# Pauses, leads and engine changes around the two branches of a hybrid encoder block

## The chip, the cores and the metric

The kernel runs on one core of a Trainium2 chip. A core has a matrix engine (TensorE, PE in the profile), three engines for elementwise work (VectorE or DVE, ScalarE or ACT, GpSimd or POOL), a SyncE (SP) that mostly issues transfers, and DMA engines that move data between memory and the core. Transfers are issued on queues of SP, ACT and POOL. The metric is the device time of one execution in microseconds; lower is better.

## The reference

One layer over a sequence of 2048 rows of width 1024, in fp32:

```python
xn = rmsnorm(x, norm1_g)
z = xn @ w_in                       # 1024 -> 4608 columns
u_pool, zq, zf, zi, zo, zg = split(z)
gates = sigmoid(zg + b_gate).reshape(B, S, 2, D_MODEL)
ya = pool_mixer(u_pool, pool_w, pool_scale) @ w_pa      # 512 -> 1024
yb = hgrn2_mixer(zq, zf, zi, zo, lb, norm_g) @ w_pb     # 512 -> 1024
x = x + (gates[:, :, 0] * ya + gates[:, :, 1] * yb) @ w_o
x = x + conv_glu_ffn(rmsnorm(x, norm2_g), w_up, conv_w, conv_b, w_down)  # 1024 -> 2 x 2816 -> 1024
return rmsnorm(x, final_g)
```

The pool mixer takes trailing means over windows of 2 to 16 rows; the HGRN2 mixer is a gated linear recurrence in chunks of 64 rows; the feed-forward part has a causal convolution of width 3 over the rows and a SiLU gate.

## The kernel before

**Precision.** Each fp32 operand is split in two parts of a shorter type, high and low: a CAST on ACT makes the high part and a subtraction on DVE the low one (L597 and L598 for activations, L205 and L206 for weights). A product is three matmuls: high by high, high by low, low by high. The names end in h and l: `mxs_1h`, `oTs_0l`, `wo_P_0l`, `m_T23h`.

**Products.** Matrix products are done in a Strassen-like form: a 2 x 2 arrangement of parts is combined to seven products P1 to P7 in place of eight. The weights for P4 to P7 are sums of parts of the weight matrix. Some of these sums are built once, in memory: class `Sums` writes, for each group of weight tiles, four matrices s1 to s4 with plain copies (issued by ACT, L278) and accumulating transfers (issued by POOL, L275), each 1 MB or less. The names su0 to su5 belong to the up projection, sd0 to sd2 to the down projection, sw0 to w_o. The generator `prepare` goes through all groups, two at a time, one transfer a step, and is driven by ticks of the matmul stream, one for six matmuls.

**Blocks.** The 2048 rows go through the program as two blocks of 1024 rows, each in two halves of 512 (hf 0 and 1). The second block runs the same code; the sums are built during the first alone. In a block the stages follow each other:

- the input projection (units of `PROJ`, seven products each), with the pooling, the recurrence and the gates beside it;
- branch pa: for each of eight column tiles m, in the order 0, 4, 1, 5, 2, 6, 3, 7, a chain of 12 matmuls for hf 0 and one for hf 1. Its moving operand is the pooled mixture `mx`, stored to memory as `md`, loaded again by SP (L796) and split to `mxs`. DVE multiplies each chain's result by a gate (L1285, L1287) to `ya`;
- branch pb: the same with the output of the recurrence (`od` to `oT` to `oTs`). DVE multiplies by the second gate (`gl`), POOL adds the product to `ya` (L1295) and then, when both halves of a row pair are there, POOL makes the combinations `yf` for P3, P5, P6 and P7 of the next product (L1084, in `add_forms`);
- wo, an object of class `Rows`: seven products of four k-steps. A step needs the split of one tile, `wo_P_k`, and each step multiplies it into four banks of PSUM. DVE adds finished banks to the rows x (L1060);
- up: 22 units of seven products (P1, P2 collect in the bank set X, P6, P7, P4 in Z, P5, P3 in V), with the convolution and the gate after each. `up_order` sets the order: P1 and P2 of two units (called heads), then of the next two, then the other products. The forms of the second half's rows (m_t, m_b, m_T11 and so on) are made by `Task`s meanwhile: transposes on PE (L646), a scaling on ACT, combinations on DVE (L703) and POOL, then splits. They may begin when product number GO_AT of up has been reached;
- down, again `Rows`, eleven k-steps for each product, with tiles reloaded from memory (`g_P`, L796 on POOL's queue), and the final norm.

**Weights.** SP loads them in order (`raw`, eight buffers); ACT and DVE split them into `ops` (six buffers, at most four ahead of use). SP's queue also carries `mx`, `oT`, the gates `gl` and more; it issues in the order of the program.

**Order on an engine.** The code is written in an order, and a scheduler with a timeline model then reorders instructions on each engine by its own estimate of when operands are ready. What each engine executes is therefore read from the printed order.

## Time and profile before

| | us |
|---|---|
| median of three runs | 2626.42 (2625.76 to 2626.61) |
| the profiled execution | 2626.91 |
| its span, first to last instruction | 2625.2 |
| PE busy, 97% of the span | 2537.5 |
| PE idle | 87.7 |
| DVE, ACT, POOL busy | 1977.9, 1170.8, 913.0 |
| mean granted clock of TensorE | 0.987 |

Rows of groups and of the timeline name the line, the engine, the operation, and out<-in by the program's names without buffer numbers. In a timeline row the first number is the start in us, the second the time it lasts, and the bracket at the end is the engine's idle time before it with what released it. ACTq and SPq are the DMA issues of ACT and SP. A matmul of 128 x 512 lasts 0.39 us but the next starts after 0.23, since they are pipelined. In the waits view a row says which engine and tile waited for which other, with total us, times, and the longest.

### The profile page before, as it was taken

What the parts mean: (1) busy time and instruction counts of PE and PEld (TensorE: products, weight loads), DVE (VectorE), ACT (ScalarE), POOL (GpSimd) and SP (SyncE); (2) the same over time, 40 slices, a digit from 0 to 9 for tenths busy, and PEclk for the clock granted to TensorE, in tenths of its full rate; (3) what the DMA queues carried; (4) which work ended last, traced back from release to release, by engine and by line L of the source; (5) the groups of instructions that cost most, each with busy time, mean ns of one, the idle gap of its engine ahead of it and who ended that gap; (6) DMA issues with size and microseconds to landing.
All of it is one profiled execution on the core that took longest, in us unless ns stands there. A gap on an engine that the chain in (4) does not pass through costs nothing. (4 is left out here: it accounts for less than half of the span.)

```text
span 2625.2 us, 35598 instructions
## 1 busy us (share of the span) xinstructions
PE 2537.5 (97%) x11464; PEld 2065.1 (79%) x11464; DVE 1977.9 (75%) x3390; ACT 1170.8 (45%) x2204; POOL 913.0 (35%) x1253
## 2 busy tenths in 40 slices
PE   7899999998999999999999999999999999999998
PEld 6688877777778888878878788888787888887887
DVE  7888779458789877877376787775778887777845
ACT  5334334313655454455364344443345454444633
POOL 6544344042444433353141111210623433335402
PEclk8999999999999999999999999999999999999999
DMA  6787759988768897488364344346452444445942
GB/s 213 271 223 205 204 181 245 267 263 209 217 184 244 239 235 211 148 299 282 98 206 159 97 125 133 109 153 213 149 166 88 151 151 148 141 140 182 378 142 105
DMA packets 254059, 496.90 MB, mean 189 GB/s; under 512 B 26736, under 2 KB 43248, under 8 KB 253552
## 3 DMA queue, kind: packets, MB, share of 16 engines
q1 hardware_dynamic: 187968, 319.89, 38.3%
q0 software_dynamic: 41504, 110.64, 16.5%
q10 hardware_dynamic: 24400, 64.08, 7.0%
q8 instruction: 91, 1.49, 0.2%
q14 instruction: 96, 0.79, 0.1%
HBM read 384.94 MB, written 187.17 MB: 218 GB/s over the span
## 5 line engine op out<-in xcount | busy, mean ns | idle before, releaser
L205 ACT CAST ops<-raw 128x512 fp32r<-128x512 f32 x732 | 451.5, 620 | 819.7 <-PE dn_P L145 140.0
L206 DVE TENSOR_TENSOR ops<-raw,ops 128x512 fp32r<-128x512 f32 x732 | 565.2, 776 | 205.3 <-ACT ops L205 194.3
L1375 DVE SCALAR_TENSOR_TENSOR e<-h,cols,e 128x512 f32<-128x512 f32 x176 | 142.6, 813 | 30.2 <-ACT e L1373 26.1
L1373 ACT ACTIVATE e<-h,cols 128x512 f32<-128x512 f32 x176 | 142.5, 814 | 24.2 <-DVE h L978 16.9
L1378 DVE SCALAR_TENSOR_TENSOR e<-h,cols,e 128x512 f32<-128x512 f32 x176 | 133.9, 769 | 3.0
L796 POOL DMA_DIRECT2D g_P<-dg_P x154 | 83.7, 545 | 107.6 <-PE dn_P L145 69.4
L1084 POOL TENSOR_TENSOR gf_P<-e,e 128x512 f32<-128x512 f32 x44 | 67.9, 1545 | 152.9 <-DVE e L1384 97.5
L1295 POOL TENSOR_TENSOR ya<-ya,gl 128x512 f32<-128x512 f32 x32 | 46.8, 1490 | 107.7 <-DVE gl L1287 107.7
L1084 POOL TENSOR_TENSOR gf_P<-gf_P,e 128x512 f32<-128x512 f32 x44 | 60.2, 1368 | 68.0 <-DVE e L1384 67.5
L1368 POOL COPY h<-h 128x2 f32<-128x2 f32 x88 | 40.7, 481 | 114.3 <-DVE h L976 112.3
L1370 POOL COPY hist<-h 128x2 f32<-128x2 f32 x88 | 35.3, 401 | 125.9 <-DVE h L978 124.2
L1382 ACT ACTIVATE e<-e 128x512 f32<-128x512 f32 x88 | 55.6, 631 | 38.8 <-DVE e L1378 38.4
L1191 POOL TENSOR_TENSOR q<-q,qs 128x512 f32<-128x512 f32 x16 | 21.9, 1366 | 141.6 <-ACT qs L1190 72.9
L978 DVE TENSOR_TENSOR h<-up_u,up_V 128x512 f32<-128x512 f32 x88 | 60.1, 684 | 13.6 <-PE up_V L145 13.1
L1228 ACT ACTIVATE gt<-gt,cols 128x512 f32<-128x512 f32 x48 | 34.8, 725 | 77.4 <-DVE gt L978 63.5
L845 POOL COPY qm<-q 128x64 f32<-128x64 f32 x64 | 24.9, 410 | 117.3 <-DVE q L910 31.2
L1060 DVE TENSOR_TENSOR x<-x,wo_P 128x512 f32<-128x512 f32 x88 | 56.6, 689 | 8.2 <-PE wo_P L145 8.2
L1060 DVE TENSOR_TENSOR ac<-ac,dn_P 128x512 f32<-128x512 f32 x72 | 46.6, 684 | 13.4 <-PE dn_P L145 13.3
L1398 POOL DMA_DIRECT2D dg_P<-gf_P x88 | 52.5, 596 | 10.8 <-POOL gf_P L1084 6.5
L853 PE MATMUL pl<-qm,k 128*128 128x192 f32 x256 | 48.2, 331 | 6.1 <-DVE qm L849 3.8
L1444 POOL TENSOR_TENSOR fss<-fss 128x1 f32<-128x1 f32 x16 | 4.6, 288 | 142.0 <-ACT fj L1433 142.0
L853 PEld LDWEIGHTS pl<-qm,k 128*128 128x128 f32 x256 | 43.3, 191 | 10.4 <-ACT qm L844 3.4
(1265 smaller groups left out, 8283.6 us busy)
## 6 DMA issues: line engine op xcount, KB each, us to landing
g_P<-dg_P POOLq DMA_DIRECT2D x154, 256.0 KB, 6.4
raw<-in_w_up_t SPq DMA_DIRECT2D x132, 256.0 KB, 3.2
raw<-in_w_in_t SPq DMA_DIRECT2D x98, 256.0 KB, 3.2
dg_P<-gf_P POOLq DMA_DIRECT2D x88, 256.0 KB, 3.9
raw<-in_w_io SPq DMA_DIRECT2D x68, 256.0 KB, 5.1
dg_P<-e SPq DMA_DIRECT2D x66, 256.0 KB, 3.3
raw<-in_w_dn SPq DMA_DIRECT2D x66, 256.0 KB, 3.0
x<-in_x SPq DMA_DIRECT2D x64, 256.0 KB, 5.3
```

The costliest lines, as they stand in the source:

```text
L205: self.mark = act.copy(hi, v)
L206: dve.tensor_tensor(lo, v, f32(hi), ALU.subtract)
L796: eng.dma_start(t, d)
L853: pe.matmul(pa_[:, c * 192 : c * 192 + 192], ks[:, (i + c) * P : (i + c + 1) * P], mv[:, c].rearrange("p s x -> p (s x)"), start=True, sto ...
L978: dve.tensor_tensor(dst, t, ps, ALU.add if how == "add" else ALU.subtract)
L1060: dve.tensor_tensor(t, t, ps[j], ALU.add if sg > 0 else ALU.subtract)
L1084: pin(pool.tensor_tensor(t, x0, x1, op))
L1373: in_turn(act.activation(t, h[:, 2:], AF.Identity, bias=col(o_cb + mt), scale=col(o_cw + 4 * MF + mt)))
L1375: in_turn(second(dve.scalar_tensor_tensor(t, h[:, 1 : 1 + TB], col(o_cw + 2 * MF + mt), t, ALU.mult, ALU.add)))
L1378: dve.scalar_tensor_tensor(t, h[:, 0:TB], col(o_cw + mt), t, ALU.mult, ALU.add)
L1382: in_turn(act.activation(g, g, AF.Silu))
L1398: pool.dma_start(d, t)
```

## The change

Six edits.

1. GO_AT is 3 in place of 5: the forms of the second half may begin two products earlier in up.
2. `up_order` leads with P1 of all four heads and then P2 of all four, where P1 and P2 came pair by pair.
3. A flag `quiet` holds `prepare`: while it is set, the generator yields without issuing. It is set when P1 of the last projection unit is through and cleared after branch pb (or when a sum is asked for that isn't done).
4. In `branch`, the first two column tiles run hf 0 of both and then hf 1 of both; the other six are as before.
5. The addition to `ya` and the four combinations `yf` in pb go to DVE; `add_forms` takes the engine as an argument. This is 32 instructions of 128 x 512 a block.
6. The `Rows` object of wo is made before pb, and the splits of P1's first three tiles are made inside pb, at its steps 3, 5 and 7.

```diff
--- before.py
+++ after.py
@@ -60,7 +60,7 @@
 N_SLOTS = 77
 N_RUN = 3
 N_HEADS = 2
-GO_AT = 5
+GO_AT = 3
 LEAD = 5
 X_AT, X_AT2 = 1, 4
 GO_IO = (("P2", 1), ("P2", 0))
@@ -283,6 +283,7 @@
             def src():
                 g, i = self.where[unit]
                 while g not in self.done:
+                    quiet[0] = False
                     prep[0].step()
                 return self.t[g, key][:, i, :]
             return src
@@ -422,7 +423,7 @@
 
     def up_order():
         heads = [(0, 1), (2, 3), (4, 5)][:N_HEADS]
-        res = [(m, p) for ms in heads for p in ("P1", "P2") for m in ms]
+        res = [(m, p) for p in ("P1", "P2") for ms in heads for m in ms]
         res += [(m, p) for ms in heads for p in ("P6", "P5", "P7", "P4", "P3") for m in ms]
 
         rest = [(7 * m + 2 * i, m, p) for m in range(2 * N_HEADS, MF)
@@ -461,7 +462,7 @@
         ms = range(m0, m0 + n + 1)
         return grouped(w_up_t, ms, [MF + m for m in ms], list(range(m0, m0 + n)))
 
-    prep = []
+    prep, quiet = [], [False]
 
     def prepare():
         todo = [sums[name].make(g) for name in ("wo", "up", "dn")
@@ -477,6 +478,8 @@
                 continue
             active.append(g)
             yield lag
+            while quiet[0]:
+                yield 1
 
     def group_rows(src, k0, n):
         v = src[k0 : k0 + n].rearrange("k p c -> p k c")
@@ -1075,13 +1078,14 @@
                         step(j, k, ws[n])
                 stream.used(hold)
 
-    def add_forms(two, forms, k, name, store=lambda p, t: None, sums=True, pin=lambda i: None):
+    def add_forms(two, forms, k, name, store=lambda p, t: None, sums=True, pin=lambda i: None,
+                  eng=pool):
 
         def comb(p, x0, x1, op):
             if (p, k) in forms or x0 is None or x1 is None:
                 return
             t = slot(f"{name}_{p}_{k}")
-            pin(pool.tensor_tensor(t, x0, x1, op))
+            pin(eng.tensor_tensor(t, x0, x1, op))
             forms[p, k] = t
             store(p, t)
 
@@ -1261,22 +1265,36 @@
                 u.multiply(p, forms, late)
                 u.after(p)
                 if n == len(PROJ) - 1 and p == "P1":
+                    quiet[0] = True
                     mtask = Task(pa_task())
 
         def branch(key, s, xs, evac, each):
-            for n, m in enumerate(M_ORDER):
-                each(n)
-                for m2 in M_ORDER[n : n + 3]:
-                    for hf in range(2):
-                        gate(s, m2, hf)
-                w4 = stream.get(key)
+            ws = {}
+
+            def chain(n, hf):
+                m = M_ORDER[n]
+                if n not in ws:
+                    each(n)
+                    for m2 in M_ORDER[n : n + 3]:
+                        for h in range(2):
+                            gate(s, m2, h)
+                    ws[n] = stream.get(key)
+                w4 = ws[n]
+                ps = bank(f"{key}{b0 + hf}_{m}")
+                chain_t(ps, lambda k: (w4[:, 0, k * P : (k + 1) * P],
+                                       w4[:, 1, k * P : (k + 1) * P]),
+                        [xs[hf, k] for k in range(4)])
+                evac(m, hf, gate(s, m, hf), ps)
+                if hf:
+                    stream.used(1)
+
+
+            for hf in range(2):
+                for n in range(2):
+                    chain(n, hf)
+            for n in range(2, len(M_ORDER)):
                 for hf in range(2):
-                    ps = bank(f"{key}{b0 + hf}_{m}")
-                    chain_t(ps, lambda k: (w4[:, 0, k * P : (k + 1) * P],
-                                           w4[:, 1, k * P : (k + 1) * P]),
-                            [xs[hf, k] for k in range(4)])
-                    evac(m, hf, gate(s, m, hf), ps)
-                stream.used(1)
+                    chain(n, hf)
 
         y, yf = {}, {}
 
@@ -1292,11 +1310,11 @@
 
         def evac_b(m, hf, g, ps):
             gated(g, hf, g, ps)
-            pool.tensor_tensor(y[m, hf], y[m, hf], g, ALU.add)
+            dve.tensor_tensor(y[m, hf], y[m, hf], g, ALU.add)
             if m >= KD // 2 and hf:
                 k = m - KD // 2
                 two = {(h, r): y[k + r * (KD // 2), h] for h in range(2) for r in range(2)}
-                add_forms(two, yf, k, f"yf{b0}")
+                add_forms(two, yf, k, f"yf{b0}", eng=dve)
 
         join(mtask)
         otask = []
@@ -1320,7 +1338,15 @@
             for c in range(2):
                 acc[hf, j, c] = xt.pop((("x", b0 + hf), j, c))
 
-        branch("pb", 1, oT, evac_b, load_res)
+        wo = Rows(f"wo{b0}", "wo", OUT, KD // 2, lambda p, k: yf[p, k], acc)
+
+        def each_b(n):
+            load_res(n)
+            if n in (3, 5, 7):
+                wo.make(n // 2)
+
+        branch("pb", 1, oT, evac_b, each_b)
+        quiet[0] = False
 
         def ready_rows(hf):
             def done(j):
@@ -1329,7 +1355,6 @@
                 ready.add((("m", b0 + hf), j))
             return done
 
-        wo = Rows(f"wo{b0}", "wo", OUT, KD // 2, lambda p, k: yf[p, k], acc)
         go_up[0] = False
         for p in ("P1", "P6", "P5"):
             wo.run(p)
```

How the orders move, at three places of block 1. First ACT, at the end of branch pa's start (mxs are the split halves of mx, gt and gd gates, sq the recurrence's norm). Before:

```order
L205 CAST ops_4963<-raw_4650 128x512
L278 DMA su1s_3386<-su1s_3384 16x16384
L791 DMA gd_0_7_4851<-gt_0_7_4849 128x512
L597 CAST mxs_0h<-mx_0_4864 128x512
L205 CAST ops_5017<-raw_4652 128x512
L278 DMA su2s_3514<-su2s_3512 16x16384
L1228 ACTIVATE gt_1_7_4876<-gt_1_7_4876,cols 128x512
L791 DMA gd_1_7_4879<-gt_1_7_4876 128x512
L597 CAST mxs_1h<-mx_1_4892 128x512
```

and now:

```order
L205 CAST ops_4962<-raw_4650 128x512
L794 DMA gd_0_7_4850<-gt_0_7_4848 128x512
L600 CAST mxs_0h<-mx_0_4863 128x512
L205 CAST ops_4986<-raw_4652 128x512
L1232 ACTIVATE gt_1_7_4875<-gt_1_7_4875,cols 128x512
L600 CAST mxs_1h<-mx_1_4891 128x512
L794 DMA gd_1_7_4878<-gt_1_7_4875 128x512
L953 ACTIVATE sq_3_4917,so_3_4918<-po_3_4908 128x128 x4
```

The copies of su1s and su2s are gone from between the casts of the second half's mx tiles; the first of them stands now after the third split of P6 in wo.

Second DVE, from the last chains of branch pb into wo (gl is the gate times the chain's result, ops a weight split, ya and yf as above). Before:

```order
L1287 TENSOR_TENSOR gl_1_7_5586<-gl_1_7_5586,pb_7_5677 128x512
L1285 SCALAR_TENSOR_TENSOR gl_1_7_5588<-gl_1_7_5588,pb_7_5697 128x512
L206 TENSOR_TENSOR ops_5772<-raw_5410,ops_5772 128x512
L598 TENSOR_TENSOR wo_P_0l<-ya_0_5004,wo_P_0h 128x512
L598 TENSOR_TENSOR wo_P_1l<-ya_1_5092,wo_P_1h 128x512
L598 TENSOR_TENSOR wo_P_2l<-ya_2_5195,wo_P_2h 128x512
L598 TENSOR_TENSOR wo_P_3l<-ya_3_5294,wo_P_3h 128x512
L598 TENSOR_TENSOR wo_P_0l<-yf_P_0_5439,wo_P_0h 128x512
```

and now:

```order
L1303 SCALAR_TENSOR_TENSOR gl_1_7_5579<-gl_1_7_5579,pb_7_5691 128x512
L206 TENSOR_TENSOR ops_5754<-raw_5380,ops_5754 128x512
L1313 TENSOR_TENSOR ya_7_5324<-ya_7_5324,gl_1_7_5579 128x512
L1088 TENSOR_TENSOR yf_P_3_5712<-yf_P_3_5710,ya_7_5324 128x512
L601 TENSOR_TENSOR wo_P_3l<-ya_3_5289,wo_P_3h 128x512
L206 TENSOR_TENSOR ops_5775<-raw_5446,ops_5775 128x512
L601 TENSOR_TENSOR wo_P_0l<-yf_P_0_5424,wo_P_0h 128x512
L601 TENSOR_TENSOR wo_P_1l<-yf_P_1_5522,wo_P_1h 128x512
L601 TENSOR_TENSOR wo_P_2l<-yf_P_2_5620,wo_P_2h 128x512
```

Before, all splits of P1 stand after the last chain's result; now `wo_P_3l` alone does, behind one addition and one combination of its own row, and those for the other tiles stand further up.

Third PE, at the start of up (m_t are the transposes of the second half's rows, up_n_X the first products of unit n). Before:

```order
L145 MATMUL up_3_X<-m_f3l,ops_6616 128x512
L145 MATMUL up_3_X<-m_f3h,ops_6616 128x512
L646 MATMUL m_t_6728<-ident,m_xs_0_6459 128x128
L646 MATMUL m_t_6728<-ident,m_xs_0_6509 128x128
L646 MATMUL m_t_6728<-ident,m_xs_0_6542 128x128
L646 MATMUL m_t_6728<-ident,m_xs_0_6581 128x128
L646 MATMUL m_t_6733<-ident,m_xs_1_6460 128x128
L646 MATMUL m_t_6733<-ident,m_xs_1_6510 128x128
L646 MATMUL m_t_6733<-ident,m_xs_1_6543 128x128
L646 MATMUL m_t_6733<-ident,m_xs_1_6582 128x128
L145 MATMUL up_2_X<-m_f4h,ops_6635 128x512
L145 MATMUL up_2_X<-m_f4l,ops_6635 128x512
```

and now:

```order
L145 MATMUL up_3_X<-m_f3l,ops_6565 128x512
L145 MATMUL up_3_X<-m_f3h,ops_6565 128x512
L649 MATMUL m_t_6680<-ident,m_xs_0_6449 128x128
L649 MATMUL m_t_6680<-ident,m_xs_0_6499 128x128
L649 MATMUL m_t_6680<-ident,m_xs_0_6532 128x128
L649 MATMUL m_t_6680<-ident,m_xs_0_6571 128x128
L649 MATMUL m_t_6685<-ident,m_xs_1_6450 128x128
L649 MATMUL m_t_6685<-ident,m_xs_1_6500 128x128
L649 MATMUL m_t_6685<-ident,m_xs_1_6533 128x128
L649 MATMUL m_t_6685<-ident,m_xs_1_6572 128x128
L145 MATMUL up_0_X<-m_f4h,ops_6592 128x512
L145 MATMUL up_0_X<-m_f4l,ops_6592 128x512
```

The same transposes lay behind both halves of units 0 and 1; now the second halves of units 0 to 3 are still to come after them.

## The prediction

> **What bounds the kernel now.** The page first, for the engine that sets the end.
>
> ```profile
> PE 2537.5 (97%) x11464; PEld 2065.1 (79%) x11464; DVE 1977.9 (75%) x3390; ACT 1170.8 (45%) x2204; POOL 913.0 (35%) x1253
> ```
>
> TensorE (PE) is busy 2537.5 of 2625.2 us and the change leaves its 11464 matmuls alone, so all that it can win lies in the 87.7 us in which PE waits, and in matmuls slowed by a lowered clock after a wait. Next the waits of PE, by what it waited for (total, times, longest).
>
> ```profile
> PE wo_P L145 <- DVE wo_P_0l L598: 7.3, 2, 6.7
> PE pa L145 <- ACT mxs_1h L597: 6.3, 1, 6.3
> PE up_Z L145 <- ACT m_T23h L597: 3.7, 2, 1.8
> PE wo_P L145 <- DVE x L1060: 3.0, 2, 1.6
> PE wo_P L145 <- ACT wo_P_0h L597: 2.5, 2, 1.2
> PE pb L145 <- ACT oTs_0h L597: 1.7, 1, 1.7
> PE up_Z L145 <- DVE m_T23l L598: 1.5, 2, 0.8
> PE pb L145 <- ACT oTs_1h L597: 1.0, 1, 1.0
> ```
>
> These eight lie where the change works: branch pa, branch pb, the start of wo, the start of up. Some come once, some twice, and the program runs its two blocks through the same code, so I put the branch stages of block 1 beside those of block 2 (window, length, busy and count of PE, PEld, DVE, ACT, POOL, then granted clock, DMA share, GB/s).
>
> ```profile
> 480.00:540.00 60.00, 53.65 (x231) 42.97 (x230) 23.05 (x42) 16.88 (x40) 4.82 (x6) 0.94 0.88 271
> 540.00:592.00 52.00, 47.88 (x196) 37.33 (x194) 33.15 (x35) 8.37 (x14) 33.48 (x26) 0.97 0.86 275
> 1757.00:1817.00 60.00, 60.00 (x294) 49.80 (x293) 30.48 (x56) 23.13 (x51) 2.41 (x4) 1.00 0.71 230
> 1822.00:1869.00 47.00, 47.00 (x204) 38.05 (x203) 24.43 (x32) 7.16 (x12) 31.47 (x24) 1.00 0.69 230
> ```
>
> In block 2 both branches run without a gap at full clock; in block 1, where alone sum matrices are built, the DMA engines are busier (0.88 and 0.86 against 0.71 and 0.69) and the clock is below 1. 47.00 us for 204 matmuls is 0.230 us a matmul, my unit below; a chain of 12 is 2.8 us.
>
> **Branch pa, block 1.** PE, then the queues that fed it.
>
> ```profile
> 489.62 0.39 PE L145 MATMUL pa<-mxs_0h,ops 128*128 128x512 f32 x1
> 496.35 0.80 PE L145 MATMUL pa<-mxs_1h,ops 128*128 128x512 f32 x1 [6.35 <-ACT mxs_1h L597]
> 500.45 0.63 PE L145 MATMUL pa<-mxs_1h,ops 128*128 128x512 f32 x1
> 501.29 0.39 PE L145 MATMUL pa<-mxs_2l,ops 128*128 128x512 f32 x1
> ```
> ```profile
> 484.78 0.47 ACTq L278 DMA_DIRECT2D su1s<-su1s  x1
> 487.54 0.47 ACTq L278 DMA_DIRECT2D su2s<-su2s  x1
> 495.68 0.62 ACT L597 CAST mxs_1h<-mx 128x512 fp32r<-128x512 f32 x1 [6.90 <-DMA mx<-md]
> 486.57 0.91 SPq L796 DMA_DIRECT2D mx<-md  x1
> ```
>
> The second half's mx tile was issued at 486.57 and cast at 495.68: 9.1 us, in company of two sum copies on ACT's queue. PE idles 6.35 us, then needs 4.94 us (496.35 to 501.29) for ten matmuls and a transpose, about 2.5 in place of 4.94, so 2.5 more: 8.9 in all. The change helps twice: the pause moves both copies behind P1 of wo, and with the first halves of two rows leading PE has one more chain (2.8 us) before it asks for the second half. Without the copies I let the load take half as long, near 4.5 us; with the 2.8 that covers 6.35 with about 1 us over. The third and fourth mx tiles follow close behind, so I leave 0.5: saved 8.4. Bounds: 2.8 if the copies were innocent, 8.9 at best.
>
> **Branch pb, block 1.**
>
> ```profile
> 545.36 0.50 PE L145 MATMUL pb<-oTs_0h,ops 128*128 128x512 f32 x1 [1.73 <-ACT oTs_0h L597]
> 549.71 0.63 PE L145 MATMUL pb<-oTs_0l,ops 128*128 128x512 f32 x1
> ```
>
> The same pattern with oT: with two short DVE waits of 0.2 each, 3.1 us idle, and again slow matmuls (0.63) after it, near 1.4 more: 4.5. Wanted 2.8 us later, two waits of 1.7 and 1.0 vanish whatever the loads do, so I take 4.5; bounds 2.8 and 4.5. The Trainium skill (TensorE: Matmul & The Clock Gate, What's actually happening) has the clock fall only after an idle window of about 3.4 us; the 0.63 rows after waits of 1.7 and 1.0 speak against that, and by it pb would be worth 3.1.
>
> **Start of wo.** Block 1 on PE, then DVE, then POOL; the last three rows are block 2 (DVE, PE, PE).
>
> ```profile
> 592.27 2.09 PE L145 MATMUL wo_P<-ops,wo_P_0h 128*128 128x512 f32 x8 [1.23 <-ACT wo_P_0h L597]
> 601.03 2.07 PE L145 MATMUL wo_P<-ops,wo_P_0l 128*128 128x512 f32 x4 [6.67 <-DVE wo_P_0l L598]
> 607.60 0.63 PE L145 MATMUL wo_P<-ops,wo_P_2h 128*128 128x512 f32 x2
> ```
> ```profile
> 592.52 8.45 DVE L598 TENSOR_TENSOR wo_P_0l<-ya,wo_P_0h 128x512 fp32r<-128x512 f32 x1
> 608.48 0.68 DVE L598 TENSOR_TENSOR wo_P_1l<-yf_P,wo_P_1h 128x512 fp32r<-128x512 f32 x1
> 609.08 0.68 DVE L598 TENSOR_TENSOR wo_P_2l<-yf_P,wo_P_2h 128x512 fp32r<-128x512 f32 x1
> ```
> ```profile
> 592.55 1.80 POOL L1084 TENSOR_TENSOR yf_P<-yf_P,ya 128x512 f32<-128x512 f32 x1
> 600.49 3.30 POOL L1084 TENSOR_TENSOR yf_P<-yf_P,ya 128x512 f32<-128x512 f32 x2
> ```
> ```profile
> 1876.76 1.77 DVE L598 TENSOR_TENSOR wo_P_1l<-ya,wo_P_1h 128x512 fp32r<-128x512 f32 x1
> 1876.89 1.19 PE L145 MATMUL wo_P<-ops,wo_P_0l 128*128 128x512 f32 x4 [0.64 <-DVE wo_P_0l L598]
> 1900.51 0.73 PE L145 MATMUL wo_P<-ops,wo_P_0h 128*128 128x512 f32 x2 [1.62 <-DVE x L1060]
> ```
>
> One split on DVE lasts 8.45 us while POOL adds without a pause; the same split lasts 0.68, one per 0.60 us, once POOL is done. In block 2 it lasts 1.77. So DVE starves beside POOL's adds, and these are what the change takes off POOL. Block 1: 1.23 + 6.67 idle, and 601.03 to 607.60 for 16 matmuls, 6.57 against 3.7: 7.9 + 2.9 = 10.8. Block 2: 1.23 + 0.64 there and 3.0 of waits for x, 4.8.
>
> What DVE takes on: 32 adds a block at 0.60 are 19.2 us. From the first product of pb to P1's last split its order now has 59 instructions, 35.4 us, against 192 matmuls or 44 us of pb, so DVE keeps pace with the chains. Three of P1's four splits stand inside pb; the last is the fifth instruction from the last chain's result, 3.0 us, and PE needs it after three steps of 12 matmuls, 8.3 us. PE's next bank demand is P5's, 22 us into wo; P1's sums end at 11, and their 16 adds with two splits take 10.8 after that where not begun earlier, which they are: about 1.8 us are over. Hidden, then, but thinly. Saved 10.8 + 4.8 = 15.6; bounds 0, if DVE falls behind by as much as it stood still, and 15.6.
>
> **Start of up, each block.** Block 1; block 2 repeats it within 0.01 us.
>
> ```profile
> 713.48 0.49 PE L145 MATMUL up_Z<-m_T23h,ops 128*128 128x512 f32 x1 [1.84 <-ACT m_T23h L597]
> 714.72 0.50 PE L145 MATMUL up_Z<-m_T23l,ops 128*128 128x512 f32 x1 [0.75 <-DVE m_T23l L598]
> 720.70 0.50 PE L145 MATMUL up_V<-m_T12l,ops 128*128 128x512 f32 x1 [0.70 <-DVE m_T12l L598]
> ```
>
> The chain to m_T23 (transposes, m_b, m_t, cast, split) may now start two products earlier, 24 matmuls or 5.5 us, more than 1.84 + 0.75. Four leading heads keep PE on operands that exist meanwhile. T12 stands behind casts and splits of weights that wait for PE's own products, so of its 0.70 I count 0.4, and 0.3 for the slow first matmuls: 3.3 a block, 6.6; bounds 3.7 (m_T23h alone) and 7.6. Later waits of up, for weights and up_u, end with PE's own products and stay.
>
> **What is paid.** The paused copies and adds are all still done. Two kinds now fall elsewhere: su3, su4 into wo and up, and the last sd1, sd2 adds among POOL's loads for down.
>
> ```profile
> g_P<-dg_P POOLq DMA_DIRECT2D x154, 256.0 KB, 6.4
> raw<-in_w_up_t SPq DMA_DIRECT2D x132, 256.0 KB, 3.2
> sd1s<-in_w_dn POOLq DMA_DIRECT2D x4, 1024.0 KB, 11.1
> ```
>
> Weight loads land in 3.2 us with eight raw tiles, eight times 2.8 us, ahead, so in up the transfers are covered by that depth. At the start of down one 11.1 us add goes out just ahead of the first seven g_P loads, on the same queue: between 0 and 11.1 - 6.4 = 4.7 us; I take 1.5, since the loads are issued ahead of need.
>
> **Sum.** 8.4 + 4.5 + 15.6 + 6.6 - 1.5 = 33.6 us. The profiled execution took 2626.91 us (span 2625.2 and 1.7 around it): 2593.3. The median of the runs is 0.5 lower, so I predict 2593. The likeliest case's own range, from part-kept pa and up to a free start of down, is 2588 to 2599.
>
> **Rivals.** (1) The loads stay late: mx's 9.1 us comes from its place on SP's queue, not from the copies. For it: in block 2, without copies, DMA is at 0.71 too. Against: block 2 has no wait. Then pa saves 2.8 and pb 2.8 in place of 12.9: 2600.
>
> (2) DVE is short at its own rate: the 1.8 us of slack in wo go, and each block waits for x at P5 and again at the next banks, 3.0 us as block 2 does now, or twice that: 2593 + 6 to 12, 2599 to 2605. For it: DVE's windows in wo are nearly full already. Against: the 0.60 us spacing.
>
> (3) Down pays: the rings work one queue off in order, so the seven g_P loads wait for the whole add: 4.7 - 1.5 = 3.2 more, twice if the sd2 add catches the next loads: 2596 to 2600. The Trainium skill (DMA: Bandwidth & Descriptors, Queues, rings and completion order) says that of one ring, while different queues share an engine packet by packet; no row of before shows an add ahead of these loads.
>
> (4) Slower: DVE stays as slow with its own adds as beside POOL's. If the 32 adds of pb cost 1.77 each, pb and P1 ask of DVE 35.4 + 32 x 1.17 = 72.8 us against 44 + 5.3 of slack: 23.5 us late a block, 47 in all, with the 15.6 of wo not won: 2593 + 15.6 + 47 = 2656. It turns slower than before once an add costs some 1.3 us. For it: two SBUF inputs as in the starved splits. Against: nothing is left on POOL in pb to starve them but DMA issues.
>
> (5) The pause is void because the sums are forced or forgotten, or the orders come out as before; then near 2625. The printed orders speak against it. A sum group late for its weights would stall SP's queue for tens of us, but the closest group stands some 19 products, 53 us, ahead of its use.
>
> **Chances.** Likeliest 0.62, (1) 0.11, (2) 0.11, (3) 0.08, (4) 0.05, (5) 0.03. What this measurement can tell from no change is 0.2%, 5.3 us. Faster: 0.62 + 0.11 + 0.11 + 0.08 = 0.92; same 0.03; slower 0.05. The range 2586 to 2609 holds the likeliest and (1) to (3), with 2 us below the sum's upper bounds and one pair of them together.
>
> **What would show it.** Right: no wait for mxs_1h over 1 us, none for oTs in block 1, wo_P_0l under 1 us, DVE's splits at 0.7 in pb, m_T23h gone from PE's waits, clock near 1 in the two windows of block 1. Wrong: x or wo_P waits at P5 (2), g_P waits at down (3), adds of 1.3 us or more on DVE (4), an mx load still at 9 us (1). The forecast falls as a whole if PE's idle time moves into wo rather than out of it.

## The result and the profile after

The changed kernel takes 2596.29 us (median of four runs, 2591.22 to 2599.39) against 2626.52 for the kernel before (four runs, 2625.76 to 2626.99): 0.9885 of it, 95% interval 0.9871 to 0.9899. The profiled execution took 2595.11 us with a span of 2593.4 and a mean granted clock of 0.993; before, 2626.91, 2625.2 and 0.987. These four executions spread over 8 us and the four of before over 1; in the later groups below, those of before spread over 9 and 10 us. The last section shows one source of it.

The engines' busy times after, from the page:

```profile
PE 2524.3 (97%) x11464; PEld 2057.6 (79%) x11464; DVE 1986.6 (77%) x3454; ACT 1170.8 (45%) x2204; POOL 823.5 (32%) x1189
```

The same 11464 matmuls take 13.2 us less, and PE's idle time falls from 87.7 to 69.1 us. DVE has its 64 instructions more. In the waits of PE after, none of the eight rows that the prediction quoted is left. These are the ones that still concern the stages it spoke of (total us, times, longest):

```profile
PE dn_P L145 <- ACT dn_P_3h L600: 3.9, 2, 2.1
PE up_V L145 <- DVE m_T12l L601: 1.8, 2, 1.3
PE dn_P L145 <- DVE dn_P_3l L601: 1.8, 1, 1.8
PE pt L965 <- DVE ot L959: 1.2, 1, 1.2
```

The two branches of block 1 after, as windows (length, busy and count of PE, PEld, DVE, ACT, POOL, then clock, DMA share, GB/s):

```profile
480.00:532.00 52.00, 50.76 (x231) 41.16 (x230) 24.56 (x45) 16.50 (x40) 3.60 (x5) 1.00 0.77 240
532.00:577.00 45.00, 45.00 (x196) 36.53 (x195) 39.59 (x64) 7.80 (x14) 0.00 (x0) 1.00 0.70 238
```

The same 231 matmuls of pa now fit in 52 us where they took 60, the 196 of pb in 45 where they took 52. The clock is 1.00, the DMA share is down to near that of block 2 before (0.71 and 0.69), and POOL does nothing in pb.

**Stage by stage.** Single times spread by some us, so the stages are compared instead. A stage begins with PE's first matmul of its bank; "lead-in" ends with the last products gr_X, and up to there PE's instructions are the same in every kernel here. The stage called pa begins there, so the projection's last products are in it too. The times are differences of starts in PE's timeline.

| stage, us | before | after | difference |
|---|---|---|---|
| block 1: lead-in | 476.15 | 475.12 | -1.03 |
| pa | 64.56 | 56.99 | -7.57 |
| pb | 51.56 | 44.43 | -7.13 |
| wo | 91.03 | 81.53 | -9.50 |
| up | 438.00 | 436.09 | -1.91 |
| down | 227.82 | 229.92 | +2.10 |
| block 2: in, gates, pa | 479.03 | 480.05 | +1.02 |
| pb | 45.98 | 44.42 | -1.56 |
| wo | 85.83 | 81.51 | -4.32 |
| up | 438.82 | 435.77 | -3.05 |
| down, to the last matmul | 218.13 | 216.38 | -1.75 |
| from gr_X to the last matmul | 2140.76 | 2107.09 | -33.67 |

The lead-in gives another 1.03, and 2.9 are lost behind the last matmul, where the last stores end later: 33.67 + 1.03 - 2.9 = 31.8, the difference of the spans. In two profiles of one kernel (the change, and the change without its part 4, were profiled twice) pa, pb, wo and up agree within 0.1 us. Between kernels whose text is the same in a stage, pa, pb and wo agree within 0.3 us, up within 2, down within 5, and the lead-in not even within 12.

Three rows after that answer to rows of before: the issue of the second half's mx on SP, its cast on ACT, and the last of P1's four splits on DVE.

```profile
483.23 0.38 SPq L799 DMA_DIRECT2D mx<-md  x1
487.17 0.62 ACT L600 CAST mxs_1h<-mx 128x512 fp32r<-128x512 f32 x1 [0.64 <-DMA mx<-md]
579.37 0.68 DVE L601 TENSOR_TENSOR wo_P_3l<-ya,wo_P_3h 128x512 fp32r<-128x512 f32 x1
```

The mx load takes 3.9 us to its cast in place of 9.1. The split, with POOL silent, takes 0.68, and so do P1's other three; before, that of wo_P_0l took 8.45.

### The profile page after: what moved, and what is told of

It reads as the page before. It is cut to its first block, busy times and chain, and to the rows that moved or that the text cites. A ratio compares the mean times of both kernels' runs of the same rounds, so it can differ in the third digit from the quotient of the medians.

```text
span 2593.4 us, 35552 instructions
## 1 busy us (share of the span) xinstructions
PE 2524.3 (97%) x11464; PEld 2057.6 (79%) x11464; DVE 1986.6 (77%) x3454; ACT 1170.8 (45%) x2204; POOL 823.5 (32%) x1189
## 4 chain that ended last, share of the span: by engine, by line
PE 68%; DVE 2%; issue 1%; DMA 1%; POOL 1%; ACT 0%; SPq 0%; DVEq 0%; POOLq 0%; ACTq 0%
PE dn_P L145 15%; PE up_Z L145 13%; PE up_V L145 9%; PE up_X L145 8%; PE wo_P L145 3%; PE gr_Z L145 3%; PE gr_V L145 2%; PE pa L145 2%; PE pb L145 2%; PE gr_X L145 2%; PE io_Z L145 1%; PE fr_Z L145 1%; PE fr_X L145 1%; PE fr_V L145 1%; PE io_V L145 1%
## 5 line engine op out<-in xcount | busy, mean ns | idle before, releaser
L206 DVE TENSOR_TENSOR ops<-raw,ops 128x512 fp32r<-128x512 f32 x732 | 552.4, 758 | 190.1 <-ACT ops L205 182.8
L1015 ACT COPY up_e<-up_X 128x512 f32<-128x512 f32 x44 | 25.8, 587 | 58.0 <-PE up_X L145 52.9
```

What stands on the lines that cost most here:

```text
L206: dve.tensor_tensor(lo, v, f32(hi), ALU.subtract)
```

## The experiments

All parts have the numbers that the description of the change gives them: 1 GO_AT, 2 `up_order`, 3 the pause, 4 the lead of two first halves, 5 the adds on DVE, 6 P1's splits inside pb. First the theory, that of the prediction: the pause frees the loads of pa and pb (12.9 us), the adds on DVE end the starvation and win wo (15.6 us), parts 1 and 2 win up (6.6 us). The rivals: the pause also wins what was credited to the adds, because wo is late through what is late in pb; or the lead, not the pause, saves pa.

Two tables gather what was measured. Times first; the kernel before was run beside each group of them.

| kernel | median us (range) | ratio to before (95%) |
|---|---|---|
| before, beside the first group | 2625.35 (2622.56 to 2631.84) | |
| only part 5 | 2633.35 (2629.42 to 2639.48) | 1.0030 (1.0018 to 1.0042) |
| all but part 5 | 2604.23 (2602.16 to 2609.97) | 0.9922 (0.9901 to 0.9943) |
| all but part 3 | 2611.77 (2607.16 to 2615.20) | 0.9946 (0.9924 to 0.9967) |
| all but part 4 | 2591.57 (2586.89 to 2593.15) | 0.9872 (0.9851 to 0.9893) |
| before, second group | 2624.68 (2619.57 to 2629.77) | |
| all but parts 1 and 2 | 2602.29 (2600.96 to 2607.87) | 0.9920 (0.9901 to 0.9940) |
| all but the splits of part 6 | 2598.11 (2595.08 to 2601.80) | 0.9901 (0.9882 to 0.9920) |
| POOL kept adding beside DVE | 2637.61 (2632.16 to 2640.72) | 1.0047 (1.0028 to 1.0066) |
| first attempt at a faster kernel | 2599.22 (2596.28 to 2601.99) | 0.9905 (0.9886 to 0.9923) |
| before, third group | 2623.70 (2619.39 to 2628.70) | |
| the change again | 2600.31 (2591.81 to 2602.55) | 0.9900 (0.9881 to 0.9919) |
| all but part 4, again | 2593.58 (2589.59 to 2598.26) | 0.9879 (0.9860 to 0.9899) |
| second attempt | 2591.41 (2586.39 to 2593.14) | 0.9871 (0.9853 to 0.9889) |
| only part 3 | 2615.91 (2612.69 to 2617.98) | 0.9968 (0.9956 to 0.9980) |

Then the stages, from each kernel's profile (b1 and b2 are the blocks; the last column is from gr_X to the last matmul):

| kernel | pa b1 | pb b1 | wo b1 | up b1 | down b1 | pb b2 | wo b2 | up b2 | all |
|---|---|---|---|---|---|---|---|---|---|
| before | 64.56 | 51.56 | 91.03 | 438.00 | 227.82 | 45.98 | 85.83 | 438.82 | 2140.76 |
| after | 56.99 | 44.43 | 81.53 | 436.09 | 229.92 | 44.42 | 81.51 | 435.77 | 2107.09 |
| only 3 | 55.52 | 45.82 | 84.72 | 441.33 | 232.21 | 45.78 | 85.31 | 438.65 | 2125.55 |
| only 5 | 64.73 | 61.23 | 90.12 | 439.74 | 228.05 | 45.84 | 81.64 | 439.38 | 2147.80 |
| all but 3 | 66.99 | 51.24 | 91.33 | 434.47 | 226.37 | 44.53 | 81.67 | 435.02 | 2129.27 |
| all but 5 | 56.99 | 44.43 | 86.55 | 435.84 | 230.11 | 44.41 | 85.27 | 434.35 | 2111.99 |
| all but 4 | 55.52 | 44.43 | 81.56 | 435.73 | 231.24 | 44.51 | 81.70 | 435.10 | 2104.84 |
| all but 1, 2 | 56.99 | 44.43 | 81.53 | 439.37 | 231.87 | 44.50 | 81.60 | 439.95 | 2115.66 |
| all but splits of 6 | 56.99 | 45.82 | 81.50 | 435.91 | 228.51 | 45.85 | 81.71 | 435.43 | 2113.15 |
| POOL beside | 56.99 | 44.43 | 102.84 | 434.94 | 233.40 | 44.38 | 102.97 | 433.78 | 2150.74 |

### Only the adds on DVE (only_dve)

Against the kernel before:

```diff
-            pool.tensor_tensor(y[m, hf], y[m, hf], g, ALU.add)
+            dve.tensor_tensor(y[m, hf], y[m, hf], g, ALU.add)
...
-                add_forms(two, yf, k, f"yf{b0}")
+                add_forms(two, yf, k, f"yf{b0}", eng=dve)
```

> The kernel before with part 5 alone: the additions of branch pb on VectorE. If VectorE was starved by POOL's additions, the long split at the start of wo (8.45 us) becomes 0.7, PE's waits for wo_P_0l and for x there go, the 1.23 us for wo_P_0h stay, and pa, pb and up keep their waits: 2626.5 - 13 = 2613 us. If VectorE is as slow with its own additions as beside POOL's, it runs late by tens of us in pb: 2630 us or more. If VectorE merely lacks time, the waits for x at P5 stay: 2616 to 2619 us.

Slower than before, by 0.3%. The time lies where the second case of the expectation put it, but not for its reason: DVE's own adds last 0.68 us. Block 2's wo won 4.2 us, as part 5 promised; block 1's won only 0.9, and pb lost 9.7. The timelines of this kernel in pb and at the start of wo (POOL, SP, ACT, PE, then DVE three times, PE):

```profile
541.31 1.16 POOL L275 DMA_DIRECT2D su3s<-in_w_up_t  x1 [34.84 <-DMA su3s<-in_w_up_t]
543.86 0.37 SPq L796 DMA_DIRECT2D oT<-od  x1
557.11 0.62 ACT L597 CAST oTs_0h<-oT 128x512 fp32r<-128x512 f32 x1 [10.05 <-DMA oT<-od]
557.78 0.80 PE L145 MATMUL pb<-oTs_0h,ops 128*128 128x512 f32 x1 [8.62 <-ACT oTs_0h L597]
592.57 0.69 DVE L1288 TENSOR_TENSOR gl<-gl,pb 128x512 f32<-128x512 f32 x1 [4.55 <-DMA gl<-gd]
606.25 0.69 DVE L1288 TENSOR_TENSOR gl<-gl,pb 128x512 f32<-128x512 f32 x1 [5.18 <-PE pb L145]
615.89 0.68 DVE L598 TENSOR_TENSOR wo_P_0l<-ya,wo_P_0h 128x512 fp32r<-128x512 f32 x1
616.63 2.08 PE L145 MATMUL wo_P<-ops,wo_P_0l 128*128 128x512 f32 x4 [7.04 <-DVE wo_P_0l L598]
```

The starvation is indeed gone: the split of wo_P_0l takes 0.68 us. Yet PE waits 7.04 us for it, because DVE comes to it late. Its in-order queue now holds the adds as well, and it stands 4.55 us before a gate that hasn't come, then another 5.18. The second wait carries PE's name, but the chain meant had ended at 597.9; a gate's load, issued at 594.32, landed at 606.16. And POOL, without the adds, is free to issue the accumulating sum transfer su3 at 541.31, which in the kernel before went out only late in pb:

```profile
580.31 1.14 POOL L275 DMA_DIRECT2D su3s<-in_w_up_t  x1
```

It now goes out 2.6 us ahead of the oT load, which needs 13.3 us (543.86 to 557.11). So relieving an engine moved the transfers queued behind it into the loads that bound the stage. That the transfer is what slows the load is inferred here from the order of the rows; the pause, below, takes such transfers away and the lateness with them.

### Only the pause (only_quiet)

Against the kernel before:

```diff
+            while quiet[0]:
+                yield 1
...
+                    quiet[0] = True
...
+        quiet[0] = False
```

> The kernel before with the pause alone. If the pause works by itself, pa and pb of block 1 lose 7 to 13 us of waits, and the starved split at wo stays, as do up and all of block 2: 2612 to 2618 us. If the pause and the additions on VectorE only work together (the additions because the gate loads come in time, the pause because VectorE is free), less than 7 us are won: 2619 us or more.

The pause alone wins 9.0 us in pa, 5.7 in pb and also 6.3 in block 1's wo, while POOL goes on adding. The time, 2615.91 us, is in the range expected, but not by its terms: the branches win more than the 7 to 13 us, and the starved split, which was to stay, does not. The first gate product of pb on DVE, POOL's first add and its last two, and the split that PE had waited for, in this kernel:

```profile
538.04 0.69 DVE L1291 TENSOR_TENSOR gl<-gl,pb 128x512 f32<-128x512 f32 x1 [2.49 <-DMA gl<-gd]
538.81 4.38 POOL L1299 TENSOR_TENSOR ya<-ya,gl 128x512 f32<-128x512 f32 x3 [49.84 <-DVE gl L1291]
581.17 3.48 POOL L1087 TENSOR_TENSOR yf_P<-yf_P,ya 128x512 f32<-128x512 f32 x2
576.58 1.78 DVE L601 TENSOR_TENSOR wo_P_0l<-ya,wo_P_0h 128x512 fp32r<-128x512 f32 x1
```

And the same first two in the kernel before:

```profile
556.37 0.68 DVE L1287 TENSOR_TENSOR gl<-gl,pb 128x512 f32<-128x512 f32 x1
557.20 2.54 POOL L1295 TENSOR_TENSOR ya<-ya,gl 128x512 f32<-128x512 f32 x2 [56.10 <-DVE gl L1287]
```

pb began at 540.71 before and at 529.66 here. So DVE's first product came 15.7 us into pb before and comes 8.4 us in now, and POOL's chain of adds starts as much earlier. But pb is 5.7 us shorter too. The chain ended 11.5 us into wo before (the prediction's row at 600.49, lasting 3.30) and ends 9.2 us into wo here; in block 2 of the kernel before it ends 9.0 us in. POOL adds beside wo's first splits in all three, so their late start alone does not explain the wait. What is gone is one long hold. Before, seven of POOL's instructions began within the 8.45 us of the split of wo_P_0l; here that split and the four after it take 1.76 to 1.80 us each, in turn with single adds, as in block 2. Before, DVE is held so long twice in block 1's pb and wo, each time just behind a sum transfer that POOL issued among its adds: the one at 580.31, quoted above, and a second (DVE, POOL):

```profile
580.66 7.62 DVE L206 TENSOR_TENSOR ops<-raw,ops 128x512 fp32r<-128x512 f32 x1
591.88 1.13 POOL L275 DMA_DIRECT2D su4s<-in_w_up_t  x1
```

With the pause POOL issues none there until its adds are done, and in block 2 none at all; there no instruction of DVE in these stages lasts over 1.85 us. That such an issue sets off the hold is suggested by the rows; no run tests it alone.

Of the 21.1 us that these three stages win, up of block 1 gives back 3.3 and down 4.4. All stages together are 15.2 us shorter; the medians differ by 0.32%, 8 us.

### All but the pause (no_quiet)

Against the change:

```diff
-                    quiet[0] = True
                     mtask = Task(pa_task())
```

> The changed kernel without the pause: the sum transfers run through the branches again. If the copies made the mx load slow, it lands in about 9 us instead of 3.9 and PE waits 2 to 4 us in pa of block 1, a lowered clock after it adds 2: 2599 to 2602 us. In pb the lead of the first halves covers the later load. If the copies are innocent, mx lands in about 4 us and nothing waits: 2596 us. If the postponed sums cost time at down, its first waits in block 1 (2.1 and 1.8 us) fall to the 1.75 us of before.

22.2 us longer in the stages than the change, and in time (2611.77 us) well above both cases of the expectation: pb and wo suffer too, which it had not counted. pa, pb and block 1's wo are as bad as before (66.99, 51.24, 91.33), though DVE adds and P1's splits stand inside pb. Waits of PE, then one row of DVE:

```profile
PE pa L145 <- ACT mxs_2h L600: 3.5, 1, 3.5
PE pb L145 <- ACT oTs_2h L600: 3.2, 1, 3.2
PE wo_P L145 <- DVE wo_P_2l L601: 3.0, 1, 3.0
```
```profile
588.00 0.69 DVE L1304 TENSOR_TENSOR gl<-gl,pb 128x512 f32<-128x512 f32 x1 [8.78 <-DMA gl<-gd]
```

With the lead, PE meets the late load one tile further on (mxs_2h for mxs_1h); no time is won. DVE waits 8.78 us for one gate, with half of pb's adds and three of P1's four splits behind it. The DMA share of such a stretch, in this kernel and then in the change (545 to 592 us):

```profile
545.00:592.00 47.00, 42.90 (x175) 33.57 (x174) 24.94 (x41) 7.25 (x12) 3.44 (x3) 0.96 1.05 292
```
```profile
545.00:592.00 47.00, 47.00 (x205) 38.18 (x205) 44.49 (x72) 14.45 (x26) 1.15 (x1) 1.00 0.61 200
```

At 1.05 the records show the DMA engines full; at 0.61 the loads come in time. What up and down gain without the pause, 1.6 and 3.6 us, is small beside it.

### All but the adds on DVE (no_dve)

Against the change:

```diff
-            dve.tensor_tensor(y[m, hf], y[m, hf], g, ALU.add)
+            pool.tensor_tensor(y[m, hf], y[m, hf], g, ALU.add)
...
-                add_forms(two, yf, k, f"yf{b0}", eng=dve)
+                add_forms(two, yf, k, f"yf{b0}")
```

> The changed kernel with the additions of pb back on POOL. If the engine is the cause, wo waits again, at its first steps or where yf is first needed, in both blocks: 2596 + 10 to 15 = 2606 to 2611 us. If the early splits of P1 inside pb are what removed the wait, at most a few us return: 2596 to 2600 us.

Only wo is longer: by 5.0 us in block 1 and 3.8 in block 2; all stages together give 4.9, since block 2's first stages and its up came out 3.6 shorter in this profile. The time, 2604.23 us, falls between the two cases of the expectation. A starved DVE instruction is still there, a weight split now (the first of the two in this row, 5.28 us; POOL had issued a sum transfer 1.6 us ahead of it), and so is PE's wait for x:

```profile
582.32 6.99 DVE L206 TENSOR_TENSOR ops<-raw,ops 128x512 fp32r<-128x512 f32 x2 [0.96 <-ACT ops L205]
```
```profile
PE wo_P L145 <- DVE x L1063: 4.2, 3, 1.9
```

Of the 10.7 us that the change won in block 1's wo, 5.0 hang on part 5 once the rest is in place, where I had credited all of them to it. The others come with the pause and with the splits in pb.

### All but the lead (no_lead, no_lead_again)

Against the change:

```diff
-            for hf in range(2):
-                for n in range(2):
-                    chain(n, hf)
-            for n in range(2, len(M_ORDER)):
+            for n in range(len(M_ORDER)):
                 for hf in range(2):
                     chain(n, hf)
```

> The changed kernel with both halves of each column tile in turn, so that PE asks for the second half 2.8 us earlier. With the pause the second mx tile is cast 3.9 us after its issue and was used 4.5 us after the cast began: 1.7 us are left, so pa waits under 1 us for it and perhaps 1 us for the third and fourth; pb waits up to 2 us for oT: 2597 to 2600 us. If the lead is what removed the waits of the branches, pa waits 2.8 us or more and the clock falls: 2601 us or more.

> The changed kernel without the leading halves, once more. If the lead costs something of its own (a wait of 1.2 us in pa for a transpose of the recurrence that came with it), this is 1 to 3 us faster than the changed kernel beside it; if the 4.7 us between the two medians so far were chance, the two agree within 1 us.

pa takes 55.52 us in both profiles, 1.47 less than with the lead, and pb the same 44.43. Neither case of the first expectation came true; the kernel is, if anything, faster. So the lead, to which the prediction gave 2.8 us of pa and most of pb, wins nothing: with the pause the second half's load is there in time without it. It costs the wait of 1.2 us for `ot` that is quoted above from the waits after and is absent here. The totals are 2104.84 and 2106.08 without it, 2107.09 and 2111.57 with it; much of that spread is block 1's down. The intervals of the times overlap (0.9872 and 0.9879 against 0.9885 and 0.9900), so only the stage is settled.

### All but the earlier forms in up (no_go)

Against the change:

```diff
-GO_AT = 3
+GO_AT = 5
...
-        res = [(m, p) for p in ("P1", "P2") for ms in heads for m in ms]
+        res = [(m, p) for ms in heads for p in ("P1", "P2") for m in ms]
```

> The changed kernel with GO_AT 5 and the old order of the heads. PE's waits for m_T23h (1.84 us) and m_T23l (0.75) return at the start of up in both blocks, and up takes 2 to 3.3 us longer in each than in the changed kernel (436.1 and 435.8 us): about 5 us in all. If the earlier start only moves the wait to m_T12l, up keeps its time within 1 us.

up is 3.3 us longer in block 1 and 4.2 in block 2, and the old waits of PE are back to the tenth:

```profile
PE up_Z L145 <- ACT m_T23h L600: 3.7, 2, 1.8
PE up_Z L145 <- DVE m_T23l L601: 1.5, 2, 0.8
```

Parts 1 and 2 are worth 7.5 us, and block 2's up is near 435 with them and near 439 without them whichever other part is left out. That agrees with the 6.6 of the prediction. The smaller 1.9 that block 1's up shows between before and after is what is left once the sums, moved there by the pause, have taken their share: 3.3 in the kernel with the pause alone.

### All but the splits inside pb (no_make)

Against the change:

```diff
         def each_b(n):
             load_res(n)
-            if n in (3, 5, 7):
-                wo.make(n // 2)
```

> The changed kernel with all splits of P1 made at wo. With only the additions moved, wo still waited 7.0 us for wo_P_0l in block 1, since the first split stood behind VectorE's last additions. If that queue is the cause, the same comes back here: the 1.23 us for wo_P_0h in both blocks and up to 6 us in block 1, wo at 83 to 88 us in place of 81.5. If the late gate load of that run was the cause, only 1.2 us come back in each block.

pb is 1.4 us longer in each block, the wait for the first cast of wo, and the other branch, wo and up don't move:

```profile
PE wo_P L145 <- ACT wo_P_0h L600: 2.5, 2, 1.2
```

Part 6 is worth 2.8 us. (The whole is 6.1 us longer in this profile; 3.7 of that lie in block 2's down, which the edit doesn't touch.) The longer queue on DVE at the start of wo did not show.

### POOL kept adding beside DVE (pool_beside)

This is the direct test of the starvation. The change is kept, and POOL repeats each add, twice, into a tile that nothing reads afterwards.

Against the change:

```diff
             dve.tensor_tensor(y[m, hf], y[m, hf], g, ALU.add)
+            for _ in range(2):
+                pool.tensor_tensor(g, g, y[m, hf], ALU.add)
```

> The changed kernel with 32 additions a block on POOL beside VectorE's own in pb; POOL's results are written over gate tiles that nobody reads any more. The output is that of the reference. If POOL's additions starve VectorE, its instructions with two SBUF inputs last 1.3 to 1.8 us or more in pb (0.68 without), VectorE falls behind the chains and wo waits in both blocks: 15 us or more in each, 2625 us or more in all. If VectorE was merely short of time, its durations stay at 0.68 and the time at 2596 us.

wo is 21.3 us longer in block 1 and 21.5 in block 2, and the kernel is 0.5% slower than before. PE's longest wait, then POOL and twice DVE in pb:

```profile
PE wo_P L145 <- DVE wo_P_3l L601: 20.4, 2, 10.2
```
```profile
555.00 6.39 POOL L1315 TENSOR_TENSOR gl<-gl,ya 128x512 f32<-128x512 f32 x4 [1.29 <-DVE ya L1313]
558.46 1.78 DVE L601 TENSOR_TENSOR wo_P_0l<-ya,wo_P_0h 128x512 fp32r<-128x512 f32 x1
560.16 0.68 DVE L1305 TENSOR_TENSOR gl<-gl,pb 128x512 f32<-128x512 f32 x1
```

While POOL adds, a DVE instruction with both inputs in SBUF (ya and wo_P_0h) takes up to 1.78 us, and one with an input in PSUM (pb) still takes 0.68. DVE's 32 adds of block 1 take 39.0 us together where they take 22.0 in the change. The price is near the one of the prediction's fourth rival, 23.5 us a block, but it needs POOL to go on. The Trainium skill (SBUF — State Buffer, Who interferes with whom) says that a DVE instruction with two SBUF inputs contends with a GpSimd instruction that reads SBUF, and that one with at most one does not, outside DVE's 2-port modes. The runs agree on which instructions suffer. How long one is held differs: here never longer than 1.8 us, about one of POOL's adds (1.3 to 1.8 us each), but 8.45 us before and 5.28 in the kernel without part 5, where several adds passed.

### Two attempts at a faster kernel (better, better2), and the change again

Both attempts leave the lead out and add to it. The first also moves POOL's two subtractions for T3 and T4 in up to DVE; both move the adds for down of up's last two units to DVE, and begin one more of down's splits ahead of it.

Against the change without the lead (the first two lines, and the same for T4, in the first attempt alone):

```diff
-                pool.tensor_tensor(t, full["B11"][k], t2, ALU.subtract)
+                dve.tensor_tensor(t, full["B11"][k], t2, ALU.subtract)
...
-                work.append((0, lambda: add_forms(have, gt, k, f"gf{b0}", store, True, in_turn)))
+                work.append((0, lambda: add_forms(have, gt, k, f"gf{b0}", store, True, in_turn,
+                                                  dve if m >= MF - 2 else pool)))
...
-        EARLY = {"P7": 2, "P4": 3}
+        EARLY = {"P7": 2, "P4": 4}
```

> The changed kernel without the leading halves, with POOL's additions for the forms of up (m_t) and those of the last two units of up on VectorE, and the fourth split of down asked for one product earlier. If starvation by POOL is what still makes PE wait for m_T12l (1.3 and 0.5 us) and for dn_P_3l (1.8), these waits go, and 2 to 4 us with them, seen in up and at the start of down: 2588 to 2590 us. If VectorE has no room left there, the waits change their names and up gets longer: 2592 us or more.

> The kernel without the leading halves, with only those of the moves of the run before that touch down: the additions of the last two units of up on VectorE and the fourth split one product earlier. There, down in block 1 took 225.7 us against 229.9 to 231.2, in block 2 nothing changed, and the loss lay in up. If that is so, up stays at 436 and 435 us and down at 226: 4 to 5 us below the kernel without the lead. If the short down was chance, the two agree.

> The changed kernel once more, beside the others on one chip. From the last product of the projection to PE's last matmul it took 2107.1 us; the same within 4 us here, whatever the stage ahead takes, whose stream is the same in all kernels and which took 469 to 482 us so far. Time 2591 to 2599 us.

The first attempt ends in the second case of its expectation, at 2599.22 us. Its up is 4.0 us longer in each block than without the lead alone (439.75 and 439.10 against 435.73 and 435.10): m_T12l no longer waits 1.3 us, but DVE's queue has grown, and two new waits stand in up:

```profile
PE up_Z L145 <- ACT m_T43h L600: 2.3, 2, 1.2
PE up_Z L145 <- ACT m_T42h L600: 2.3, 2, 1.2
```

The second attempt, without these subtractions, has block 1's down at 227.56 us against 231.24 and 231.86, and the lowest total of all, 2101.98. Its time, 2591.41 us, is level with the kernel without the lead (2591.57, 2593.58) and below both runs of the change (2596.29, 2600.31), with overlapping intervals; that it is faster than the change is likely, but only the stages show it.

The change run again misses its expectation on both counts: 2111.57 us in the stages, 4.5 more than 2107.1, all of it in the two down stages, and 2600.31 us in time.

Its rows show what is paid at down. In the change run again, POOL, then ACT, DVE, ACT and PE:

```profile
1082.09 1.19 POOL L275 DMA_DIRECT2D sd1s<-in_w_dn  x1
1087.54 3.80 POOL L799 DMA_DIRECT2D g_P<-dg_P  x7
1094.96 1.18 POOL L275 DMA_DIRECT2D sd2s<-in_w_dn  x1 [3.62 <-DMA sd1s<-in_w_dn]
1095.83 0.62 ACT L600 CAST dn_P_0h<-g_P 128x512 fp32r<-128x512 f32 x1 [2.53 <-DMA g_P<-dg_P]
1096.48 1.75 DVE L601 TENSOR_TENSOR dn_P_0l<-g_P,dn_P_0h 128x512 fp32r<-128x512 f32 x1 [2.46 <-ACT dn_P_0h L600]
1108.32 0.63 ACT L1407 ACTIVATE e<-e 128x512 f32<-128x512 f32 x1 [2.11 <-DVE e L1403]
1109.51 3.27 PE L145 MATMUL dn_P<-ops,dn_P_3h 128*128 128x512 f32 x8 [3.95 <-ACT dn_P_3h L600]
```

In the kernel without the pause the last such add is 104 us ahead of down, and PE waits less:

```profile
1015.60 1.21 POOL L275 DMA_DIRECT2D sd2s<-in_w_dn  x1
1130.23 2.13 PE L145 MATMUL dn_P<-ops,dn_P_3h 128*128 128x512 f32 x8 [1.75 <-ACT dn_P_3h L600]
```

The pause moves the last two sum adds to 15 and 2 us before down starts. The first of them goes out 5.4 us ahead of the seven g_P loads and lands 12.6 us after its issue; the first load lands 1.0 us after it, 8.20 us after its own issue, where it takes 4.37 without the pause. In each of the eleven profiles with the pause the first load lands 1.0 to 1.5 us after that add. ACT and DVE stand some 2.5 us for this load, the last unit's work behind it comes late, ACT reaches the cast of dn_P_3h late (it stands behind `e`), and PE waits 3.95 us for it in place of 1.75. POOL's own 3.62 us, before the second add may be issued, hold up the last adds for down; what that costs the rows don't separate. In the second attempt the wait on dn_P_3h is gone, and one of 1.2 us, on dn_P_4h, stands in its place: its fourth split, moved one product earlier, is cast ahead of that `e`. What moving the adds to DVE gave beside that was not tested alone.

## Why the prediction was right, and where it was wrong

The time, 2593 forecast and 2596.29 measured, and the sum, 33.6 forecast and 33.67 in the stages, agree. That the sums agree so closely is luck: the terms miss by -1.64 to +1.40 us and the misses cancel, and the change run again gave 29.19 in the stages.

| us saved in | forecast (bounds) | measured |
|---|---|---|
| pa, block 1 | 8.4 (2.8 to 8.9) | 7.57 |
| pb, block 1, without wo_P_0h's 1.23 | 4.5 (2.8 to 4.5) | 5.90 |
| wo, block 1, with wo_P_0h's 1.23 | 10.8 | 10.73 |
| pb and wo, block 2 | 4.8 | 5.88 |
| up, both blocks | 6.6 (3.7 to 7.6) | 4.96 |
| down, block 1 | -1.5 (-4.7 to 0) | -2.10 |
| down of block 2; rest of block 2 | none | +1.75; -1.02 |

- **pa.** Right in size and cause as to the copies: the load takes 3.9 us where I had estimated 4.5. Wrong on "the change helps twice": the lead's 2.8 us aren't needed, and it costs 1.47.
- **pb.** The step that mis-sized it is the one that allowed 1.4 us for slow matmuls after waits of 3.1 us in all; 5.90 - 3.1 = 2.8 went that way. The bound of 4.5 was too low, since it took that 1.4 as certain. The granted clock stood at 0.50 from 549.06 to 552.48, though PE had been busy for 1.98 of the 3.41 us before. The rule of the Trainium skill that I set beside it (TensorE: Matmul & The Clock Gate, What's actually happening), a clock that falls only after an idle window of some 3.4 us, gave 3.1; the measurement is farther from it still.
- **wo.** The size held and the credit did not. The failing step is "these are what the change takes off POOL" with "Saved 10.8 + 4.8": it put the starved split down to the adds' engine alone. Alone the adds on DVE win 0.9 us in block 1, and the pause alone, with POOL still adding, wins 6.3. I had set the split's 8.45 us in block 1 beside its 1.77 in block 2 and did not ask why the same split beside the same adds is held so much longer in the one; block 1 is where the sum transfers run. In block 2, where none run, the credit was right (4.2 us for the adds alone).
- **DVE's new load.** "Hidden, then, but thinly" holds where gates come in time. It fails without the pause: PE then waits 7.04 us in wo for an operand that stands behind gate loads on DVE. The prediction counted DVE's instructions against PE's chains and left out what DVE itself waits for. Nor did it ask what POOL issues once freed: "nothing is left on POOL in pb to starve them but DMA issues" named them, and their effect on the loads was the larger one, 9.7 us in pb.
- **up.** Block 2 gave 3.05 of the 3.3 forecast, block 1 only 1.91. Without the pause block 1 gains 3.5 too, so the pause costs 1.6 there. In the rows m_T12l's wait grew from 0.70 to 1.26: its splits stand behind one that POOL stretches. DVE, POOL, PE after:

```profile
685.95 3.59 DVE L206 TENSOR_TENSOR ops<-raw,ops 128x512 fp32r<-128x512 f32 x1
685.94 3.05 POOL L740 TENSOR_TENSOR m_t<-m_b,m_t 128x512 f32<-128x512 f32 x2
692.60 0.50 PE L145 MATMUL up_V<-m_T12l,ops 128*128 128x512 f32 x1 [1.26 <-DVE m_T12l L601]
```

- **down.** The one pair of profiles gives -2.10. Over all profiles, nine with the pause (the attempts left out) have a mean of 231.4 us and three without it 227.4, so what is paid is 3.9, nearer the third rival's 4.7 than my 1.5. The failing step is "I take 1.5, since the loads are issued ahead of need": the loads land 1.9 to 3.9 us later behind the add, and PE's wait for dn_P_3h grows by up to 2.2 us.
- **Rivals.** (1) loads late in any case: false, 3.9 us. (2) DVE short at its own rate: false, no wait for x is left in wo. (3) came true in its order, the loads landing behind the add, and near its size, and moved the total by 2.4 us only. (4) false in the change, where DVE's adds take 0.69; its price, 21 us a block, comes when POOL really goes on. (5) false.

Left open: why a DVE instruction beside POOL's adds sometimes takes its turn after one of them (1.78 us) and sometimes after several (8.45, 7.62, 5.28, 3.59 us). Each of these four stands 0.4 to 1.6 us behind a sum transfer issued by POOL, but other such issues pass without a hold. Open too is how much of down's 3.9 us is POOL's wait and how much the loads behind the add.

## What to carry to other kernels

Work that moves from one engine to another takes with it the place of everything queued behind it: the freed engine issues its transfers earlier, and the loaded one puts its other duties behind the new work's operands. So parts of a change should be priced alone and within the whole: here, in the stages, the adds won 5 us with the rest in place and lost 7 alone. Where small loads bound a stage, look first at which bulk transfers share it and can wait, and at where they land when they are let go. And where the same code runs twice, ask of every wait that only one of the passes shows what that pass alone contains.

## What the runs showed of the hardware that was not expected

The lead-in, with the same instructions on PE in all kernels, took from 468.93 to 481.51 us. Over the 14 profiles PE's idle time in it is 33.9 to 37.5 us, and its busy time on the same 2104 matmuls 434.4 to 444.2: most of the difference lies in how fast the same matmuls ran and not in the waits (the granted clock over it was 0.964 to 0.985). One stretch of it, 200 to 265 us, in the kernel without parts 1 and 2, and then in the one without part 4:

```profile
200.00:265.00 65.00, 60.81 (x296) 50.25 (x295) 53.27 (x125) 26.35 (x64) 28.28 (x30) 0.95 0.74 197
```
```profile
200.00:265.00 65.00, 62.55 (x319) 52.09 (x318) 57.08 (x133) 26.45 (x64) 31.86 (x31) 1.00 0.81 218
```

In the first, 23 matmuls fewer are done in the same 65 us, at a clock of 0.95. It contains this wait, with slow matmuls behind it:

```profile
252.84 1.62 PE L856 MATMUL pl<-qm,k 128*128 128x192 f32 x4 [3.16 <-DVE qm L852]
```

PE idled only 1.7 us more in the first. Matched one by one in PE's order, its matmuls run 3.4 us behind the second kernel's at the start of the stretch and 8.3 at the end, so some 3 of the 4.9 us lost went in slower matmuls. The times of one kernel within the three groups of runs spread by 5 to 11 us; the lead-in alone is enough for that, and a part worth 3 us is seen in the stages and not in the median.
